# Gated-MLP layer's values: 128-column weight blocks stationary, or token tiles stationary with 512 weight columns moving

## The chip, the cores and the metric

The kernel runs on one core of one Trainium2 chip. The metric is the device time of one execution in microseconds (us). One execution is also recorded by the hardware profiler; its span, from the first to the last instruction of the program, is what the profile's times are measured in.

## The reference, cut to what matters

The reference is one inference step of a two-layer decoder trunk for a prompt group (256 tokens) and a sample group (8 sequences of 8 tokens), 320 tokens in all, `D_MODEL` 1024, in float32. The first layer is a chunked gated MLP:

```python
def chunk_spatial_gating(x, w_in, ln_g, ln_b, w_s, b_s, w_out):
    h = jax.nn.gelu(x @ w_in)                 # w_in: 1024 x 4096
    u, v = jnp.split(h, 2, axis=-1)           # 2048 columns each
    ... # v: layer norm over its 2048 columns
    mixed = jnp.einsum('gts,bnsgd->bntgd', ws, vc) + b_s[:, :L].T[:, :, None]
    y = (u * mixed.reshape(bsz, s, D_A)) @ w_out
    return y, v
```

`x` has been through an RMS norm. The change concerns `v`, the second half of `x @ w_in`: 320 tokens by 2048 columns, 1024 deep. `v` is wanted with tokens on partitions, since the layer norm runs along its columns and the mixing over tokens contracts it. Behind this layer stand a gated convolution MLP, an mLSTM layer and a second convolution MLP; they are not changed.

## The kernel before, in words

**Precision by parts.** A float32 product is made of three float32r matmuls. Each operand is split into a high part (a cast to float32r) and a low part (what is left): `wh`, `wl` of a weight block, `xh`, `xl` of the activations. The products high by high, high by low and low by high are added in PSUM.

**Weights.** All weights are queued by `weights()` in the order of use, as pieces of up to 8 tiles of 128 x 128. `take()` hands out the next piece; `prefetch(n, m)` issues the loads up to piece n (SyncE's queue, SP, into one of 4 `raw` buffers) and the splits up to piece m (ScalarE, ACT, casts `wh`; VectorE, DVE, subtracts to make `wl`; 3 buffers each). Loads run 4 pieces ahead, splits one.

**A block.** `block()` computes 128 output columns for all tokens: for each of the 8 k tiles it calls `self.mm` (L47) three times with a 128 x 128 weight tile stationary and 320 token columns moving, into one PSUM bank `pm` (pool `psm`, 3 banks). TensorE (PE) instructions are pinned in program order; a scheduler places the rest.

**The start.** `run()` loads the activations `xT` (128 partitions x 8 x 320) in four transfers of two k tiles, each followed by a piece of the first weight block (2, 2 and 4 k tiles, then 4 of the second block). After each, `norm_block` makes `xh` and `xl`: the square root of the mean is not yet known, so the parts are of x times the norm's gain, and the row factor `rc` is applied after the matmul. Ten matmuls on ones (`pw`) stand ahead. The squares for the norm follow in block 1, `norm_cols` (row factor by token, `rc`) in block 3, `norm_row` (the same as a row, `rb`) in block 5, `row_sums` in block 10.

**The values.** Sixteen blocks, weight columns 2048 to 4095. Each result has columns on partitions, and is turned: DVE copies it from PSUM to `vT`, and one block later `v_nat` transposes three token tiles (128, 128, and the last 128 tokens, of which the upper 64 are the sample) on PE into `pvt` (three banks of the pool `psa`, which has 5). After four blocks ACT applies gelu with `rc` as scale into `v`, and DVE takes `bn_stats` for the layer norm. The last transposes stand after the first u block.

**After that.** Sixteen blocks for `u`, with the normalising of `v` and the mixing (`mix`) between them, then the output projection.

Of the kernel before, what the change touches and what calls it, by code (L numbers as in the profile page):

```python
# [22 lines left out]
KD = D // P  # L23
DA = 2048
# [9 lines left out]
V_MIX, V_FFN, V_FIN, V_GN, V_LG, V_LB, V_CB, V_FB, V_FW, V_CW = 0, 16, 32, 40, 56, 72, 88, 104, 148, 280  # L34
# [3 lines left out]
class Net:  # L38
# [23 lines left out]
    def weights(self):  # L62

        I = self.I
        q = []

        def add(w, b, *groups, k0=0):
            for kn in groups:
                q.append((w, b, k0, kn))
                k0 += kn  # L70

        add(I["a_win"], 16, 2, 2, 4)
        add(I["a_win"], 17, 4, 4)
        for b in [*range(18, 32), *range(16)]:
            add(I["a_win"], b, 8)
        for b in range(KD):
            add(I["a_wo"], b, 8, 8)

        def ffn(l):
            for b in range(2 * KF):  # L80
                add(I["f_up"][l], b, 8)
            for b in range(KD):
                add(I["f_dn"][l], b, 8, 7, 7)

        ffn(0)
        add(I["b_wg"], 0, 8)
        for h in range(NH):
            for r in range(6):
                if (h, r) == (NH - 1, 4):
                    add(I["b_wo"], 0, 4, k0=8)  # L90
                    add(I["b_wo"], 1, 6, k0=8)
                add(I["b_win"], 6 * h + r, 8)
                for b in self.EARLY_OUT.get((h, r), ()):
                    add(I["b_wo"], b, 8)
        add(I["b_wo"], 2, 6, k0=8)
        add(I["b_wo"], 0, 4, k0=12)
        for b in (1, 2):
# [10 lines left out]
    def prefetch(self, n, m):  # L108

        nc = self.nc  # L110
        while len(self.loaded) < min(n, len(self.wq)):
            w, b, k0, kn = self.wq[len(self.loaded)]
            raw = self.wraw.tile([P, 8, P], F32, tag="raw", name="raw")
            nc.sync.dma_start(raw[:, :kn, :], w[b, :, k0:k0 + kn, :])
            self.loaded.append(raw)
        while len(self.halved) < min(m, len(self.wq)):
            i = len(self.halved)
            raw, kn = self.loaded[i], self.wq[i][3]
            self.loaded[i] = None
# [9 lines left out]
            self.last_split = nc.scalar.copy(wh[:, :kn, :], raw[:, :kn, :])  # L129
            self.last_low = nc.vector.tensor_tensor(wl[:, :kn, :], raw[:, :kn, :], wh[:, :kn, :].bitcast(F32), op=SUB)  # L130
            self.halved.append((wh, wl))
# [89 lines left out]
    def norm_row(self):  # L221
# [13 lines left out]
        nc.scalar.copy(rb, pb[:, :T])  # L235
        self.rb = rb

    def x_rhs(self, k):
        return self.xh[:, k, :], self.xl[:, k, :]

# [14 lines left out]
    def layer_a(self):  # L255
        nc, tc, I, O = self.nc, self.tc, self.I, self.O
        with tc.tile_pool(name="ya", bufs=1) as yp, tc.tile_pool(name="la", bufs=1) as lp:
            yh = yp.tile([P, KA, T], F32R, name="yh_a")
            yl = yp.tile([P, KA, T], F32R, name="yl_a")
            v = lp.tile([P, 3, DA], F32, name="v_a")  # L260
            st = lp.tile([P, 3, 4, 6], F32, name="st_a")
            mv = lp.tile([P, 3, 2], F32, name="mv_a")
# [6 lines left out]
            pvt = {}  # L269

            def load_ws():
                nc.sync.dma_start(ws, I["a_ws"])
# [11 lines left out]
                    self.mm(pr, self.ones, ws[:, 4 * i:4 * i + 4, :], True, True)  # L284
                    nc.scalar.copy(rsum[:, 4 * i:4 * i + 4, :].rearrange("p g t -> p (g t)"), pr)

            def v_nat(b, vT):
                q, c = b // 4, b % 4
                if c == 0:
                    pvt[q] = [self.psa.tile([P, 512], F32, tag="pa", name="pvt") for _ in range(3)]  # L290
                for t in range(3):
                    self.tr(pvt[q][t][:, c * P:(c + 1) * P], self.tokens(vT, t), self.ident)
                if c == 3:
                    for t in range(3):
                        vv = v[:, t, q * 512:(q + 1) * 512]
                        nc.scalar.activation(vv, pvt[q][t], AF.Gelu_apprx_tanh, scale=self.rc[:, t:t + 1])
                        nc.vector.bn_stats(st[:, t, q, :], vv)

            prev = None
            for b in range(16):  # L300
                ps = self.block(KD, self.x_rhs)
                if b == 1:
# [3 lines left out]
                if b == 3:  # L306
                    self.norm_cols()
                    load_ws()
                if b == 5:
                    self.norm_row()  # L310
                if b == 10:
                    row_sums()
                if prev is not None:
                    v_nat(b - 1, prev)
                prev = lp.tile([P, T], F32, tag="vT", name="vT", bufs=2)
                nc.vector.tensor_copy(prev, ps[:, :T])

            ve = lp.tile([P, 3], F32, name="ve_a")
            rs = lp.tile([P, 3], F32, name="rstd_a")

            def v_stats():
                for t in range(3):
                    nc.vector.bn_aggr(mv[:, t, :], st[:, t])
                nc.vector.tensor_scalar(ve, mv[:, :, 1], EPS, None, op0=ADD)
                nc.gpsimd.tensor_tensor(rs, ve, self.mhalf.to_broadcast([P, 3]), op=ALU.pow)
                nc.vector.scalar_tensor_tensor(ve, mv[:, :, 0], -1.0, rs, op0=MULT, op1=MULT)

            def normalise(q):
                for t in range(3):
                    vv = v[:, t, q * 512:(q + 1) * 512]  # L330
                    nc.scalar.activation(vv, vv, AF.Identity, scale=rs[:, t:t + 1], bias=ve[:, t:t + 1])

            def v_rows(q):
                cs = slice(q * 512, (q + 1) * 512)
# [30 lines left out]
            for b in range(16):  # L365
                ps = self.block(KD, self.x_rhs)
                if b == 0:
                    v_nat(15, prev)
# [596 lines left out]
    def run(self):  # L965
        nc, tc, I, O = self.nc, self.tc, self.I, self.O
        with tc.tile_pool(name="const", bufs=1) as cp, tc.tile_pool(name="xp", bufs=1) as xp, \
# [6 lines left out]
            self.xh = xp.tile([P, KD, T], F32R, name="xh")  # L974
# [11 lines left out]
            for i in range(10):  # L986
                self.mm(pw[:, :P], self.ones, self.ones, True, True)
            nc.sync.dma_start(self.vecs[:, :16], I["vecs"][:, :16])
            for i in range(4):
                nc.sync.dma_start(self.xT[:, 2 * i:2 * i + 2, :], I["xT"][:, 2 * i:2 * i + 2, :])  # L990
                self.prefetch(i + 1, 0)
                for m in (2 * i, 2 * i + 1):
                    self.norm_block(m, V_MIX)
                self.prefetch(i + 1, min(i + 1, 3))
            nc.sync.dma_start(self.ident, I["ident"])
            nc.sync.dma_start(self.vecs[:, 16:], I["vecs"][:, 16:])
            self.layer_a()
            self.ffn(0, V_MIX + 8)
            self.layer_b()
# [15 lines left out]
def _lay_out(i):  # L1015
    a = {}
# [5 lines left out]
    a["a_win"] = _blocks(i["a_w_in"][0])  # L1022
# [16 lines left out]
    w = i["b_w_in"][0]  # L1039
# [68 lines left out]
```

## Time and profile before

| | |
|---|---|
| median of 3 runs | 977.2 us (976.13 to 979.38) |
| profiled execution | 977.89 us, its span 975.8 us |
| mean granted TensorE clock in it | 0.994 |
| PE busy | 957.5 us (98%) |
| DVE busy | 686.7 us (70%) |
| ACT busy | 484.6 us (50%) |
| first matmul of the first value block | 5.57 us |
| first matmul of the first u block | 73.27 us |

How to read the profile: PE is the matmul engine, PEld its weight loads, which overlap the matmuls. A row of the timeline gives the start, the length, the engine, the line of the kernel, the operation, `out<-in` by tile names, the shapes and a count. PE's records of neighbouring matmuls overlap, so the pace of a stream is read from start to start. In a row of grouped instructions the numbers behind the bar are busy time, mean ns of one, and the idle time of the engine ahead of them with what ended it. A float32 matmul that is not a transpose shows as two records. A row of the windows gives the stretch, its length, busy time and count by engine, the granted clock, the mean busy share of the DMA engines and GB/s.

### The profile page before, as it was taken

Reading aid. Unit: us, or ns where it says so; the run is one execution under the profiler, and the core shown is the slowest. Engines: PE = TensorE matmul, PEld = TensorE weight load, DVE = VectorE, ACT = ScalarE, POOL = GpSimd, SP = SyncE. Lnnn points to the kernel's source line nnn. Section 1 sums busy time; section 2 is a strip of 40 time slices with the busy share of each in tenths; the row PEclk is TensorE's granted clock in tenths of the full one; section 3 lists DMA queues with packets and bytes.
Section 4 is the critical chain, followed back from the end, with each engine's and each line's share of the span. In section 5 each row is a group of like instructions: output and inputs, shape, how many; then the busy total and the mean of one; then the engine's idle time right before and its main releaser. Section 6 shows DMA issues by size and latency. Waiting matters only on the chain. (4 is left out here: it accounts for less than half of the span.)

```text
span 975.8 us, 17507 instructions
## 1 busy us (share of the span) xinstructions
PE 957.5 (98%) x6703; PEld 941.0 (96%) x6703; DVE 686.7 (70%) x1344; ACT 484.6 (50%) x846; POOL 71.9 (7%) x238
## 2 busy tenths in 40 slices
PE   9999999999999999999989999999999999999996
PEld 8999999999999999999889999999899999999996
DVE  6647985577777764548988887787787777775442
ACT  6437444445554543347456665464565455544332
POOL 0200000010000000012200110011001000000000
PEclk9999999999999999999999999999999999999999
DMA  8534434434444445553854556545273444444441
GB/s 283 193 119 159 140 133 155 152 133 149 151 152 151 148 147 152 150 190 101 279 188 156 189 174 221 170 160 164 73 239 137 152 152 151 152 146 149 147 129 54
DMA packets 55944, 154.73 MB, mean 159 GB/s; under 512 B 6758, under 2 KB 17638, under 8 KB 55862
## 3 DMA queue, kind: packets, MB, share of 16 engines
q1 hardware_dynamic: 55862, 153.62, 47.4%
q8 instruction: 53, 0.87, 0.4%
q14 instruction: 29, 0.24, 0.1%
HBM read 141.66 MB, written 11.94 MB: 157 GB/s over the span
## 5 line engine op out<-in xcount | busy, mean ns | idle before, releaser
L129 ACT CAST wh<-raw 128x1024 fp32r<-128x1024 f32 (+3 forms) x254 | 257.4, 1014 | 353.0 <-PE pm L47 221.9
L47 PE MATMUL pm<-xh,wh 128*128 128x320 f32 x1344 | 422.7, 315 | 1.2 <-ACT wh L129 1.2
L47 PE MATMUL pm<-xh,wl 128*128 128x320 f32 x1344 | 417.5, 311 | 0.1
L47 PE MATMUL pm<-xl,wh 128*128 128x320 f32 x1344 | 417.0, 310 | 0.0
L130 DVE TENSOR_TENSOR wl<-raw,wh 128x1024 fp32r<-128x1024 f32 (+3 forms) x254 | 300.2, 1182 | 124.5 <-ACT wh L129 122.4
L47 PEld LDWEIGHTS pm<-xh,wh 128*128 128x128 f32 x1344 | 253.9, 189 | 2.4 <-ACT wh L129 1.6
L47 PEld LDWEIGHTS pm<-xh,wl 128*128 128x128 f32 x1344 | 253.6, 189 | 0.7 <-DVE wl L130 0.7
L47 PEld LDWEIGHTS pm<-xl,wh 128*128 128x128 f32 x1344 | 253.9, 189 | 0.2
L47 PE MATMUL pm<-yh_f,wh 128*128 128x320 f32 x352 | 109.1, 310 | 0.0
L47 PE MATMUL pm<-yl_f,wh 128*128 128x320 f32 x352 | 108.6, 309 | 0.0
L47 PE MATMUL pm<-yh_f,wl 128*128 128x320 f32 x352 | 108.6, 309 | 0.0
L47 PEld LDWEIGHTS pm<-yl_f,wh 128*128 128x128 f32 x352 | 66.2, 188 | 0.0
L47 PEld LDWEIGHTS pm<-yh_f,wh 128*128 128x128 f32 x352 | 66.1, 188 | 0.0
L47 PEld LDWEIGHTS pm<-yh_f,wl 128*128 128x128 f32 x352 | 66.1, 188 | 0.0
L420 DVE SCALAR_TENSOR_TENSOR fcv<-fpad,vecs,fcv 128x336 f32<-128x336 f32 x88 | 49.6, 566 | 2.2 <-ACT fcv L418 0.7
L243 DVE TENSOR_TENSOR xT<-pm,xT 128x320 f32<-128x320 f32 x40 | 19.6, 491 | 41.6 <-PE pm L47 41.4
L47 PE MATMUL pm<-yhb,wh 128*128 128x320 f32 x128 | 40.3, 315 | 0.2 <-ACT yhb L839 0.2
L47 PE MATMUL pm<-ylb,wh 128*128 128x320 f32 x128 | 39.6, 310 | 0.4 <-DVE ylb L840 0.4
L47 PE MATMUL pm<-yhb,wl 128*128 128x320 f32 x128 | 39.5, 309 | 0.5 <-DVE wl L130 0.5
L47 PE MATMUL pm<-yh_a,wh 128*128 128x320 f32 x128 | 39.6, 309 | 0.0
L47 PE MATMUL pm<-yl_a,wh 128*128 128x320 f32 x128 | 39.5, 309 | 0.0
L47 PE MATMUL pm<-yh_a,wl 128*128 128x320 f32 x128 | 39.5, 309 | 0.0
(241 smaller groups left out, 1116.1 us busy)
## 6 DMA issues: line engine op xcount, KB each, us to landing
raw<-in_f_up SPq DMA_DIRECT2D x88, 512.0 KB, 3.2
raw<-in_b_win SPq DMA_DIRECT2D x48, 512.0 KB, 3.6
raw<-in_a_win SPq DMA_DIRECT2D x30, 512.0 KB, 3.2
raw<-in_f_dn SPq DMA_DIRECT2D x32, 448.0 KB, 3.3
C<-in_C SPq DMA_DIRECT2D x32, 258.0 KB, 5.3
raw<-in_a_wo SPq DMA_DIRECT2D x16, 512.0 KB, 3.7
raw<-in_f_dn SPq DMA_DIRECT2D x16, 512.0 KB, 3.4
out_Cs<-C SPq DMA_DIRECT2D x32, 256.0 KB, 3.9
```

The source lines that it names most:

```text
L47: self.pin(self.nc.tensor.matmul(out, lhsT, rhs, start=start, stop=stop))
L129: self.last_split = nc.scalar.copy(wh[:, :kn, :], raw[:, :kn, :])
L130: self.last_low = nc.vector.tensor_tensor(wl[:, :kn, :], raw[:, :kn, :], wh[:, :kn, :].bitcast(F32), op=SUB)
L243: self.nc.vector.tensor_tensor(x, ps[:, :T], x, op=ADD)
L420: nc.vector.scalar_tensor_tensor(cv, pd[:, i:i + NC], self.vec(w + i * KF), cv, op0=MULT, op1=ADD)
```

## The change

The operands of the value product change places. A tile of 128 tokens of `xh` or `xl` is stationary, and 512 columns of the weights move, so that the result has tokens on partitions and needs no transposes. There are four groups of 512 columns. In a group, for each k tile, two prompt tiles take three matmuls each. The 64 sample tokens take two: `xh` holds behind its 320 token columns a copy (by GpSimd, POOL) of the sample's `xl`, so that 128 stationary columns are the sample's high and low parts side by side (`xs`); they take `wh`. The high 64 alone take `wl`, into the same lower half of the bank. ACT then copies the lower 64 rows of the bank to SBUF, and DVE adds the upper 64. A group holds two banks of `psa` and one of `psm`; gelu reads them as `pvt` before.

The value weights have a layout of their own, `a_wv` (group, partition, k tile by four column tiles), and are taken by k: in the first group 8 pieces of one k tile, in the others 4 pieces of two. At the start `bring` loads `xT` in eight transfers of one k tile, each followed by its weight piece, and `enter` makes that k tile's `xh`, `xl` and copy, while the first group is under way. The loads run no further ahead than that (`AHEAD` 0) until the last x. The squares follow the first group, `norm_cols` and the first group's gelu stand in the middle of the second, `norm_row` after the second, `row_sums` after the third; the statistics for the sample are taken on partitions 64 to 127 alone.

```diff
-        add(I["a_win"], 16, 2, 2, 4)
-        add(I["a_win"], 17, 4, 4)
-        for b in [*range(18, 32), *range(16)]:
+        for g in range(4):
+            add(I["a_wv"], g, *(1,) * 8 if g == 0 else (2,) * 4)
+        for b in range(16):
             add(I["a_win"], b, 8)
...
+    def bring(self, n):
+        nc, I = self.nc, self.I
+        for m in range(self.brought, min(n, KD)):
+            nc.sync.dma_start(self.xT[:, m, :], I["xT"][:, m, :])
+            self.prefetch(m + 1, 0)
+            if m == KD - 1:
+                nc.sync.dma_start(self.ident, I["ident"])
+                nc.sync.dma_start(self.vecs[:, 16:], I["vecs"][:, 16:])
+                self.AHEAD = Net.AHEAD
+        self.brought = max(self.brought, min(n, KD))
+
+    def enter(self, m):
+        self.norm_block(m, V_MIX)
+        self.nc.gpsimd.tensor_copy(self.xx[:, m, T:], self.xl[:, m, TP:])
...
-            def v_nat(b, vT):
-                q, c = b // 4, b % 4
-                if c == 0:
-                    pvt[q] = [self.psa.tile([P, 512], F32, tag="pa", name="pvt") for _ in range(3)]
-                for t in range(3):
-                    self.tr(pvt[q][t][:, c * P:(c + 1) * P], self.tokens(vT, t), self.ident)
-                if c == 3:
...
+            def columns(q, k, pv, wh, wl):
+                xs = self.xx[:, k, TP:TP + P]
+                for t in range(2):
+                    xh, xl = self.tokens(self.xh[:, k, :], t), self.tokens(self.xl[:, k, :], t)
+                    self.mm(pv[t], xh, wh, k == 0, False)
+                    self.mm(pv[t], xl, wh, False, False)
+                    self.mm(pv[t], xh, wl, False, k == KD - 1)
+                if k == 0:
+                    self.mm(pv[2], xs, wh, True, False)
+                self.mm(pv[2][:64], xs[:, :64], wl, False, False)
+                if k > 0:
+                    self.mm(pv[2], xs, wh, False, k == KD - 1)
+
+            def v_gelu(q, pv):
+                cs = slice(q * 512, (q + 1) * 512)
+                r = slice(64, P)
+                vs = lp.tile([P, 512], F32, tag="vs", name="vs", bufs=2)[r]
+                nc.scalar.copy(vs, pv[2][:64])
+                nc.vector.tensor_tensor(vs, vs, pv[2][r], op=ADD)
+                for t in range(2):
+                    nc.scalar.activation(v[:, t, cs], pv[t], AF.Gelu_apprx_tanh, scale=self.rc[:, t:t + 1])
+                    nc.vector.bn_stats(st[:, t, q, :], v[:, t, cs])
+                nc.scalar.activation(v[r, 2, cs], vs, AF.Gelu_apprx_tanh, scale=self.rc[r, 2:3])
+                nc.vector.bn_stats(st[r, 2, q, :], v[r, 2, cs])
+
+            waiting = None
+            for q in range(4):
+                pv = [self.psa.tile([P, 512], F32, tag="pa", name="pv") for _ in range(2)] + \
+                    [self.psm.tile([P, 512], F32, tag="pm", name="pvs")]
+                k = 0
+                while k < KD:
+                    if q == 0:
+                        self.bring(k + 4)
+                        if k + 1 < KD:
+                            self.enter(k + 1)
+                    (wh, wl), kn = self.take()
+                    wh, wl = [x.rearrange("p (k e) c -> p k (e c)", e=4) for x in (wh, wl)]
+                    for i in range(kn):
+                        columns(q, k + i, pv, wh[:, i, :], wl[:, i, :])
+                    k += kn
+                    if q == 1 and k == 4:
+                        self.norm_cols()
+                        v_gelu(0, waiting)
...
-            for i in range(4):
-                nc.sync.dma_start(self.xT[:, 2 * i:2 * i + 2, :], I["xT"][:, 2 * i:2 * i + 2, :])
-                self.prefetch(i + 1, 0)
-                for m in (2 * i, 2 * i + 1):
-                    self.norm_block(m, V_MIX)
-                self.prefetch(i + 1, min(i + 1, 3))
...
+            self.AHEAD, self.brought = 0, 0
+            self.bring(3)
+            self.enter(0)
+            self.prefetch(1, 1)
```

More of the change, by code (lines that the diff above doesn't have):

```diff
@@ L113, in prefetch @@
             raw = self.wraw.tile([P, 8, P], F32, tag="raw", name="raw")
-            nc.sync.dma_start(raw[:, :kn, :], w[b, :, k0:k0 + kn, :])
+            if w is self.I["a_wv"]:
+                kn *= 4
+                nc.sync.dma_start(raw[:, :kn, :], w[b, :, 4 * k0:4 * k0 + kn, :])
+            else:
+                nc.sync.dma_start(raw[:, :kn, :], w[b, :, k0:k0 + kn, :])
             self.loaded.append(raw)
@@ L118, in prefetch @@
             raw, kn = self.loaded[i], self.wq[i][3]
+            if self.wq[i][0] is self.I["a_wv"]:
+                kn *= 4
             self.loaded[i] = None
@@ L268, in layer_a @@
             bdt = lp.tile([P, 64], F32, name="bdt")
-            pvt = {}
             def load_ws():
@@ L285, in row_sums @@
                     nc.scalar.copy(rsum[:, 4 * i:4 * i + 4, :].rearrange("p g t -> p (g t)"), pr)
-            def v_nat(b, vT):
-                q, c = b // 4, b % 4
-                if c == 0:
-                    pvt[q] = [self.psa.tile([P, 512], F32, tag="pa", name="pvt") for _ in range(3)]
-                for t in range(3):
-                    self.tr(pvt[q][t][:, c * P:(c + 1) * P], self.tokens(vT, t), self.ident)
-                if c == 3:
[L294 to L302, printed above, removed]
+            nc.gpsimd.memset(v[:64, 2, :], 0.0)
+            nc.gpsimd.memset(mv[:64, 2, :], 0.0)
+            def columns(q, k, pv, wh, wl):
[10 more added lines that the diff above has]
+                    self.mm(pv[2], xs, wh, False, k == KD - 1)
@@ new lines, in layer_a @@
+            waiting = None
[16 more added lines that the diff above has]
+                        v_gelu(0, waiting)
+                if q == 0:
@@ L305, in layer_a @@
                             self.square_block(m)
-                if b == 3:
-                    self.norm_cols()
+                if q == 1:
+                    self.norm_row()
                     load_ws()
-                if b == 5:
-                    self.norm_row()
-                if b == 10:
+                if q == 2:
                     row_sums()
[L313 to L316, printed above, removed]
+                if q > 0:
+                    v_gelu(q, pv)
+                waiting = pv
             ve = lp.tile([P, 3], F32, name="ve_a")
@@ L322, in v_stats @@
                 for t in range(3):
-                    nc.vector.bn_aggr(mv[:, t, :], st[:, t])
+                    r = slice(64 if t == 2 else 0, P)
+                    nc.vector.bn_aggr(mv[r, t, :], st[r, t])
                 nc.vector.tensor_scalar(ve, mv[:, :, 1], EPS, None, op0=ADD)
@@ L329, in normalise @@
                 for t in range(3):
-                    vv = v[:, t, q * 512:(q + 1) * 512]
-                    nc.scalar.activation(vv, vv, AF.Identity, scale=rs[:, t:t + 1], bias=ve[:, t:t + 1])
+                    r = slice(64 if t == 2 else 0, P)
+                    vv = v[r, t, q * 512:(q + 1) * 512]
+                    nc.scalar.activation(vv, vv, AF.Identity, scale=rs[r, t:t + 1], bias=ve[r, t:t + 1])
             def v_rows(q):
@@ L973, in run @@
             self.xT = xp.tile([P, KD, T], F32, name="xT")
-            self.xh = xp.tile([P, KD, T], F32R, name="xh")
+            self.xx = xp.tile([P, KD, TP + P], F32R, name="xh")
+            self.xh = self.xx[:, :, :T]
             self.xl = xp.tile([P, KD, T], F32R, name="xl")
@@ L988, in run @@
             nc.sync.dma_start(self.vecs[:, :16], I["vecs"][:, :16])
-            for i in range(4):
-                nc.sync.dma_start(self.xT[:, 2 * i:2 * i + 2, :], I["xT"][:, 2 * i:2 * i + 2, :])
-                self.prefetch(i + 1, 0)
-                for m in (2 * i, 2 * i + 1):
-                    self.norm_block(m, V_MIX)
-                self.prefetch(i + 1, min(i + 1, 3))
-            nc.sync.dma_start(self.ident, I["ident"])
-            nc.sync.dma_start(self.vecs[:, 16:], I["vecs"][:, 16:])
+            self.AHEAD, self.brought = 0, 0
+            self.bring(3)
+            self.enter(0)
+            self.prefetch(1, 1)
             self.layer_a()
@@ L1021, in _lay_out @@
                                "f_conv_w", "b_conv_w")], axis=1))
-    a["a_win"] = _blocks(i["a_w_in"][0])
+    a["a_win"] = _blocks(i["a_w_in"][0][:, :DA])
+    a["a_wv"] = np.ascontiguousarray(
+        i["a_w_in"][0][:, DA:].reshape(KD, P, 4, 4, P).transpose(2, 1, 0, 3, 4)).reshape(4, P, 4 * KD, P)
     a["a_wo"] = _blocks(i["a_w_out"][0])
```

1 line of the change is left out of this document (removed).

## The prediction

> **What bounds the kernel now.** I read the page first, then the busy windows of the stage that is rewritten, then its timeline.
>
> ```profile
> span 975.8 us, 17507 instructions
> PE 957.5 (98%) x6703; PEld 941.0 (96%) x6703; DVE 686.7 (70%) x1344; ACT 484.6 (50%) x846; POOL 71.9 (7%) x238
> 5.57:12.72 7.15, 5.88 (x24) 0.76 0.98 343
> 57.87:61.72 3.85, 3.85 (x30) 1.00 0.14 47
> 80.72:84.24 3.52, 3.52 (x27) 1.00 0.32 120
> ```
>
> TensorE (PE) is busy for 98% of the span. The three windows (length, PE busy, records touched, granted clock, DMA share, GB/s) are the first value block, a later one, and a block of the first half of a_w_in (u block). The later blocks have no idle PE at full clock; the first takes twice as long, with idle time and a clock of 0.76. So two things can change the end: how many PE slots the values need, and how the start is fed. A matmul's record overlaps the next, so I count from start to start.
>
> ```profile
> 57.63 0.49 PE L50 MATMUL pvt<-ident,vT 128*128 128x128 f32 x3
> 57.87 0.40 PE L47 MATMUL pm<-xh,wh 128*128 128x320 f32 x1
> ...
> 61.72 0.39 PE L47 MATMUL pm<-xh,wh 128*128 128x320 f32 x1
> ...
> 73.27 0.39 PE L47 MATMUL pm<-xh,wh 128*128 128x320 f32 x1
> ...
> 80.72 0.31 PE L47 MATMUL pm<-xh,wh 128*128 128x320 f32 x1
> ...
> 84.24 0.31 PE L47 MATMUL pm<-xh,wh 128*128 128x320 f32 x1
> ```
>
> A u block of 24 matmuls of 320 columns takes 84.24 - 80.72 = 3.52 us, 146.7 ns each. A value block has three transposes more and takes 61.72 - 57.87 = 3.85, so the transposes cost 0.33. The last value block ends at 73.27.
>
> **Steady part: removed.** Sixteen blocks at 3.85 us go: 61.6 us of PE, of which 56.3 are 384 matmuls and 5.3 the 48 transposes. Sixteen copies of vT on VectorE (DVE) go too; PE never waited for them in the steady blocks, so they count nothing.
>
> **Steady part: added.** Four groups of 8 k steps of 8 matmuls, 256 in all, each with 512 moving columns. In columns it is a draw: 256 x 512 = 131,072 against 384 x 320 + 48 x 128 = 129,024. What decides is the cost that does not grow with the columns, paid 256 times and not 432. No float32r matmul of 512 columns is in this trace; I extrapolate from 258 and 320.
>
> ```profile
> 502.24 0.28 PE L47 MATMUL num<-vh,Ph 128*128 128x258 f32 x1
> ...
> 503.56 0.28 PE L47 MATMUL pCp<-vh,kgl 128*128 128x258 f32 x1
> ```
>
> Eleven starts of 258 columns lie between 502.24 and 503.56: 120 ns each. The step to 320 costs 26.7 ns for 62 columns, 0.43 ns a column, so 512 columns cost 146.7 + 192 x 0.43 = 229 ns. Lower bound: the flattest slope that the rounding of those two starts allows (121 ns at 258 columns, 0.415 a column) gives 226. Upper bound: in proportion to columns, 146.7 x 1.6 = 235. I take 229, nearest to the two measured float32r rows: 256 x 0.229 = 58.6 us, a gain of 3.0 (1.4 to 3.7).
> The Trainium skill, "TensorE: Matmul & The Clock Gate", section "Back-to-back issue gap", has a gap of N / 2.4 + 2.5 ns, 216 ns for 512; by it the sum would be 3.4 us lower. It gives 136 ns for 320 columns where the trace has 146.7, so the measurement decides.
>
> Row sums, norm_cols and norm_row keep their matmuls, only between other instructions. The weight bytes and the cast and subtract of each weight tile stay; ScalarE (ACT) gets four 64-row copies and loses nothing large, DVE four 64-row adds. What covers them:
>
> ```profile
> 20.00:73.30 53.30, 53.30 (x369) 52.01 (x367) 31.27 (x47) 21.36 (x28) 4.98 (x3) 1.00 0.50 167
> L296 ACT ACTIVATE v_a<-pvt,rc 128x512 f32<-128x512 f32 x9 | 5.5, 683 | 0.0
> ```
>
> In this stage DVE is busy 31.27 of 53.30 us and ACT 21.36, under a PE that is full. The exposed place is a group's turn. A group takes two banks of psa, which has five; with the banks of the norms and row sums between, the second token tile of groups 2 and 3 reuses the bank of the first tile of the group before, and waits for its gelu. That bank is complete five matmuls (1.15 us) before the group ends; the gelu is 0.68 us (L296), and the built order puts it ahead of the sample's copy on ACT. It is done before it is wanted, so I count nothing; if ACT is late by a weight cast as well, two turns cost up to 1.3 us each.
>
> **The start.** Now to the feed.
>
> ```profile
> 4.21 1.01 ACT L174 ACTIVATE xh<-xT,vecs 128x320 fp32r<-128x320 f32 x2 [1.92 <-DMA xT<-in_xT]
> 5.57 0.41 PE L47 MATMUL pm<-xh,wh 128*128 128x320 f32 x1
> 6.76 0.31 PE L47 MATMUL pm<-xh,wl 128*128 128x320 f32 x1
> 6.87 1.01 ACT L174 ACTIVATE xh<-xT,vecs 128x320 fp32r<-128x320 f32 x2 [1.35 <-DMA xT<-in_xT]
> 8.23 0.41 PE L47 MATMUL pm<-xh,wh 128*128 128x320 f32 x1 [1.17 <-ACT wh L129]
> ...
> 2.00:4.00 2.00, 2.00 (x11) 1.00 0.83 221
> 4.00:6.00 2.00, 1.99 (x11) 1.00 0.95 274
> 6.00:8.00 2.00, 0.98 (x5) 1.00 0.96 351
> 8.00:10.00 2.00, 1.75 (x6) 0.65 1.06 381
> 10.00:12.00 2.00, 2.00 (x10) 0.50 0.92 321
> L129 ACT CAST wh<-raw 128x512 fp32r<-128x512 f32 x3 | 1.8, 608 | 0.5 <-DMA raw<-in_a_win 0.5
> L130 DVE TENSOR_TENSOR wl<-raw,wh 128x512 fp32r<-128x512 f32 x3 | 2.0, 682 | 0.0
> ```
>
> The first block takes 7.15 us where 3.52 would do: 3.63 us lost, because two k steps of x feed only six matmuls (0.9 us) and the next x lands at 6.87, and because after that pause the clock is granted at half (0.65, 0.50) until about 12. Now each k step has 8 matmuls of 229 ns, 1.83 us of PE, and needs 164 KB of x and 262 KB of weights: 0.43 MB. By the GB/s column 0.44 MB have come by 4 us, 0.99 by 6, 1.69 by 8, 2.45 by 10 and 3.10 by 12. So 0.43 MB take 1.1 to 1.6 us: the feed is faster than PE, where before it was slower. Step by step: x and weights 0 land as now, so the first matmul starts at 5.6; its third waits for wl until about 6.2, and step 0 ends at 7.6. Pair 1 is in at about 7.3: its 0.87 MB have come by 5.6, and a landing lags behind its bytes (the x used at 6.87 was the end of 0.79 MB, which had come by 5.3, a lag of 1.5). Cast 0.61 and subtract 0.68 make 8.6, and six matmuls more end step 1 near 10.0. From there PE is the limit: six steps of 1.83, end 21.0. Without loss it would be 5.57 + 14.66 = 20.2: 0.8 us lost instead of 3.6, a gain of 2.8. Upper end 3.4, when pair 1 is in at 6.7. Lower end 1.2, when the clock is still granted at half for one stretch like that before, 3.1 us, at a cost of half, 1.6.
> The eight x transfers and eight weight transfers stand on SP's queue where nine stood; its issue is under 0.5 us each, 1 us per step, below 1.83. GpSimd copies 64 columns of xl per step, wanted only after the six prompt matmuls, so that is covered.
>
> **Sum.** -3.0 - 2.8 = -5.8 us. The profiled execution took 977.89 (span 975.8), which becomes 972.1; the median of the three runs is 977.2, 0.7 lower, so 971.4. For this case alone 970 to 974.6.
>
> **Rivals.** First, the one that ends slower: the 64-wide stationary. Where the shape of the stationary changes, PE does not overlap:
>
> ```profile
> 494.72 0.31 PE L47 MATMUL pm<-xh,wl 128*128 128x320 f32 x1
> 494.96 1.08 PE L47 MATMUL num<-C,Qz 128*32 128x258 f32 x16
> ```
>
> The 32-wide matmul starts 0.24 us after the 320-column one instead of 0.147, 0.07 before the record's end. A record grows from 0.28 (258) to 0.31 (320), so to 0.40 at 512; the next would start after 0.33, not 0.229: 0.10 us a change. The 32 matmuls that load only xs[:, :64] stand each between 128-wide ones: 64 changes, 6.2 us, net +0.4: 977.6. It decides if over 58 of 64 changes pay. Against it: in the built program these loads are 64 wide but still select all four column groups of the array, as the 128-wide ones do, while the loads of num select one. I give it 0.12.
> The Trainium skill, "TensorEngine Tiling (Array Packing)", "Key Properties", says that changing the tiling mode drains TensorE, and the row agrees, with 0.09 us. "PSUM — Partial Sum Buffer", "The four PSUM rules", of the same skill says that float32r matmuls force the column group to all; no run here shows that yet.
>
> Second, the start stays as lossy as it is: x in single steps and more transfers land no earlier, the clock drops, 3.6 us are lost again. For it: the half clock in the rows above. Against it: the bytes. Time 977.2 - 3.0 = 974.2; chance 0.12. Third, the turns, two of 1.3 us: 971.4 + 2.6 = 974.0, or 976.8 if the start is lossy as well. For it: PE then waits in program order, with everything behind. Against it: the order of the gelus and the idle share of ACT. Chance 0.08. That the change doesn't do what it says (the transposes stay, say) is excluded by the built order: 256 matmuls of 512 columns and no transposes in this stage.
>
> **Numbers.** Forecast 0.68, the switch 0.12, the start 0.12, the turns 0.08. A measurement here tells about 0.3%, 2.9 us, from no change. Below 974.3 lie 0.65 of the forecast's 0.68 and just under half of the start and the turns together (0.09 of 0.20): faster 0.74. Within 0.3% lie the upper edge of the forecast, the rest of those two, and most of the switch, 0.08: same 0.20 (0.03 + 0.09 + 0.08). A switch with a lossy start, 977.6 + 2.8 = 980.4, is slower: 0.04, and 0.02 for a start and turns beyond their prices: 0.06. The range leaves out the switch and reaches from 969.8, 0.3 under the forecast's low end for the spread of runs, to the turns with a lossy start, 976.8.
>
> **What would show it.** Starts of 512-column rows 226 to 235 ns apart, first u block at 67 to 69 us instead of 73.27, the first group over at 21, no clock of 0.5 at 8 to 12. Wrong if rows next to the 64-wide ones start 0.33 apart (switch), if group 0 ends after 23 (start), or if PE waits for ACT at the start of group 2 or 3 (turns).

## The result, and the profile after

The changed kernel takes 970.58 us (median of 4 runs, 970.23 to 972.09) where the kernel before takes 977.18 (976.13 to 979.38): a ratio of 0.9933, 95% interval 0.9919 to 0.9947. The forecast was 971.4. The profiled execution took 970.37, with a span of 968.6.

The first lines of the page, and then one row from the busy windows of PE (length, PE busy, records) for the first group, 5.63 to 21.20:

```profile
span 968.6 us, 17160 instructions
PE 951.8 (98%) x6527; PEld 922.9 (95%) x6527; DVE 684.6 (71%) x1333; ACT 489.8 (51%) x851; POOL 75.1 (8%) x248
5.63:21.20 15.57, 15.57 (x66) 11.56 (x66) 9.34 (x16) 9.35 (x17) 2.62 (x7) 1.00 0.95 306
```

PE is as full as before; 5.7 us of its busy time are gone. In the first group, where the old first block stood idle and half-clocked, the window counts no idle PE and a clock of 1.00. Its start is not free of loss all the same: the first two steps take 4.55 us, two later ones 3.67.

The timeline of PE, start of the first group, then a later step, then the start of the second group and the end of the stage:

```profile
5.63 0.60 PE L47 MATMUL pv<-wh,xh 128*128 128x512 f32 x1
6.06 0.40 PE L47 MATMUL pv<-wh,xl 128*128 128x512 f32 x1
6.35 0.50 PE L47 MATMUL pv<-wl,xh 128*128 128x512 f32 x1
...
7.97 0.50 PE L47 MATMUL pv<-wh,xh 128*128 128x512 f32 x1
8.31 0.40 PE L47 MATMUL pv<-wh,xl 128*128 128x512 f32 x1
8.70 0.50 PE L47 MATMUL pv<-wl,xh 128*128 128x512 f32 x1
...
10.18 0.39 PE L47 MATMUL pv<-wh,xh 128*128 128x512 f32 x1
...
14.55 0.39 PE L47 MATMUL pv<-wh,xh 128*128 128x512 f32 x1
14.78 0.39 PE L47 MATMUL pv<-wh,xl 128*128 128x512 f32 x1
15.01 0.39 PE L47 MATMUL pv<-wl,xh 128*128 128x512 f32 x1
15.23 0.40 PE L47 MATMUL pvs<-wl,xh 128*64 128x512 f32 x1
15.47 0.39 PE L47 MATMUL pvs<-wh,xh 128*128 128x512 f32 x1
15.70 0.40 PE L47 MATMUL pv<-wh,xh 128*128 128x512 f32 x1
...
21.20 0.40 PE L47 MATMUL pv<-wh,xh 128*128 128x512 f32 x1
21.43 0.40 PE L47 MATMUL pv<-wh,xl 128*128 128x512 f32 x1
22.01 0.50 PE L47 MATMUL pv<-wl,xh 128*128 128x512 f32 x1 [0.18 <-DVE wl L136]
...
68.41 0.39 PE L47 MATMUL pvs<-wh,xh 128*128 128x512 f32 x1
68.64 0.31 PE L47 MATMUL pm<-xh,wh 128*128 128x320 f32 x1
```

Step 0 ends at 7.97 and step 1 at 10.18; from there a step takes 1.83 to 1.84 us, 229 ns from start to start. The row behind the 64-wide stationary starts 0.24 after it, the others 0.22 to 0.23. Behind the first steps, one wait for weights is visible, at 22.01: the first weights of the second group are split late, and the two starts around it are 0.58 apart, not 0.23. The first group is over at 21.20, and the first u block begins at 68.64 (73.27 before).

**Where the 7.2 us of span went.** The stage gives 4.63, and 0.33 more because no transposes stand behind the first u block: 5.0. At the first matmul of the output projection the changed kernel leads by as much, 135.65 against 140.68, and it holds that lead for 295 us:

```profile
140.68 0.40 PE L47 MATMUL pm<-yh_a,wh 128*128 128x320 f32 x1
```

```profile
135.65 0.39 PE L47 MATMUL pm<-yh_a,wh 128*128 128x320 f32 x1
```

The next 1.6 come at the turn from the first convolution MLP to the mLSTM layer, which the change does not touch: the lead is 5.0 in front of it and 6.6 behind. The timeline of PE there, of the kernel before:

```profile
433.37 0.61 PE L47 MATMUL pc<-ones,acc 128*128 128x2 f32 x4
435.22 0.58 PE L47 MATMUL pc<-ones,acc 128*128 128x2 f32 x2 [1.24 <-DVE acc L210]
435.67 0.61 PE L47 MATMUL pm<-xh,wh 128*128 128x320 f32 x1
436.08 0.47 PE L47 MATMUL pm<-xl,wh 128*128 128x320 f32 x1
...
438.72 0.31 PE L47 MATMUL pm<-xh,wl 128*128 128x320 f32 x1
438.87 0.31 PE L47 MATMUL pm<-xh,wh 128*128 128x320 f32 x1
```

and of the changed kernel:

```profile
428.33 0.61 PE L47 MATMUL pc<-ones,acc 128*128 128x2 f32 x4
430.19 0.38 PE L47 MATMUL pc<-ones,acc 128*128 128x2 f32 x2 [1.25 <-DVE acc L216]
430.43 0.39 PE L47 MATMUL pm<-xh,wh 128*128 128x320 f32 x1
430.66 0.31 PE L47 MATMUL pm<-xl,wh 128*128 128x320 f32 x1
```

Both pause for the same 1.24 or 1.25 us. Behind the pause, the kernel before runs at 267 ns a matmul instead of 147 until 438.7, and the changed kernel does not. The busy window over that stretch shows a granted clock of 0.50:

```profile
435.26:438.68 3.42, 3.42 (x13) 3.42 (x14) 0.89 (x5) 1.04 (x1) 0.85 (x1) 0.50 0.84 271
```

The last 0.6 come at the first `num<-C` matmuls, whose wait for the transfer of C is that much shorter in this trace. It is not a part of the change: the stretch that holds this wait, from the matmuls that spread the row factor (`pb`) to the second start of `pcs`, takes 57.10 us in the kernel before and 56.53 in the changed kernel here, but 57.26 in a second trace of the changed kernel and 56.94 and 57.68 in two traces of the kernel before with a filled pause elsewhere. So the stage accounts for 5.0 of the 7.2 us of span, and 2.2 were made elsewhere.

The time of an execution is longer than its span, and by less in the changed kernel: by 1.7 to 1.8 us in each of its ten unaltered runs, against 2.0 to 2.1 in the runs of the kernel before. These 0.3 us are a part of the measured gain that no trace shows; what makes them stays open.

### The profile page after: what moved, and what is told of

Read it like the earlier page. It is cut to its first block, busy times and chain, and to the rows that moved or that the text cites. A ratio compares the mean times of both kernels' runs of the same rounds, so it can differ in the third digit from the quotient of the medians.

```text
span 968.6 us, 17160 instructions
## 1 busy us (share of the span) xinstructions
PE 951.8 (98%) x6527; PEld 922.9 (95%) x6527; DVE 684.6 (71%) x1333; ACT 489.8 (51%) x851; POOL 75.1 (8%) x248
## 5 line engine op out<-in xcount | busy, mean ns | idle before, releaser
L47 PE MATMUL pm<-xh,wh 128*128 128x320 f32 x1216 | 379.6, 312 | 0.0
L47 PE MATMUL pm<-xh,wl 128*128 128x320 f32 x1216 | 375.8, 309 | 0.0
L47 PE MATMUL pm<-xl,wh 128*128 128x320 f32 x1216 | 375.7, 309 | 0.0
L47 PEld LDWEIGHTS pm<-xh,wh 128*128 128x128 f32 x1216 | 228.4, 188 | 0.8
L47 PEld LDWEIGHTS pm<-xl,wh 128*128 128x128 f32 x1216 | 228.4, 188 | 0.3
L47 PEld LDWEIGHTS pm<-xh,wl 128*128 128x128 f32 x1216 | 228.2, 188 | 0.0
```

The source lines that it names most:

```text
L47: self.pin(self.nc.tensor.matmul(out, lhsT, rhs, start=start, stop=stop))
```

## The experiments

The ratios are against the kernel before, run on the same chip beside them (977.75 us for the first four experiments, 976.26 for the next four, 977.65 for the last two). My theory: a fixed cost for each matmul makes the steady part cheaper, and transfers in single k steps that each feed 1.83 us of PE make the start cheaper. The rivals: fine transfers alone do it; the 64-wide stationary costs much; the rest of the 6.6 us belongs to the change as well.

**Coarse start.** `xT` in four transfers of two k tiles, the first group's weights in four pieces of two; the parts of two k tiles are made ahead of each piece.

```diff
-            add(I["a_wv"], g, *(1,) * 8 if g == 0 else (2,) * 4)
+            add(I["a_wv"], g, *(2,) * 4)
...
-            nc.sync.dma_start(self.xT[:, m, :], I["xT"][:, m, :])
-            self.prefetch(m + 1, 0)
+            nc.sync.dma_start(self.xT[:, m:m + 2, :], I["xT"][:, m:m + 2, :])
+            self.prefetch(m // 2 + 1, 0)
```

> The changed kernel, but x comes in four transfers of two k tiles and the first group's weights in four pieces of two k tiles (512 KB), as the old start had its x. The products are the new ones. Theory (the start's gain needs both, small first steps and more PE work for each byte of x): the first pair is 0.33 MB of x and 0.52 MB of weights, in at about 7.2 us instead of 4.9; the first matmul comes at 8.2 instead of 5.63, the first group ends at 23.6 to 25.5 instead of 21.20 (the upper end if the clock is granted at half for one stretch of 3.4 us after the pause), and the whole is 2.4 to 4.3 us slower than the changed kernel: 973 to 975. Rival (the new products alone repair the start, since PE then has 1.8 us of work per k step): the first group still ends by 22, 970.6 to 971.4.

974.67 us, ratio 0.9966 (0.9954 to 0.9978). The timeline of PE:

```profile
7.79 0.79 PE L47 MATMUL pv<-wh,xh 128*128 128x512 f32 x1 [2.00 <-ACT wh L135]
...
10.06 0.63 PE L47 MATMUL pv<-wh,xl 128*128 128x512 f32 x1
10.49 0.63 PE L47 MATMUL pv<-wl,xh 128*128 128x512 f32 x1
...
25.55 0.40 PE L47 MATMUL pv<-wh,xh 128*128 128x512 f32 x1
```

The first matmul waits 2.2 us longer, for the larger first weight piece; then a stretch runs 0.43 us a matmul, the pace of half clock, until 13.8. The clock column of the windows has 1.00 there, so it does not show this stretch. The first group is over at 25.55 instead of 21.20, 4.35 later; the first u block starts at 72.52, 3.9 later, since the weight wait of 22.01 is absent. Without the fine steps the new blocks lose the whole 2.7 of the start and 1.7 us more, half of it as a later first matmul, the rest in the slow stretch.

**Fine start, old blocks.** The kernel before, with `xT` in eight transfers and the first block's weights in eight pieces of one k tile.

```diff
-        add(I["a_win"], 16, 2, 2, 4)
+        add(I["a_win"], 16, *(1,) * 8)
...
+    def first_block(self):
+        ps = self.psm.tile([P, 512], F32, tag="pm", name="pm")
+        for k in range(KD):
+            self.bring(k + 4)
+            if k + 1 < KD:
+                self.norm_block(k + 1, V_MIX)
+            self.chunk(ps, lambda j: self.x_rhs(k + j), k == 0, k == KD - 1)
+        return ps
```

> The kernel before, its sixteen blocks and transposes unchanged, but fed as the changed one: x in eight transfers of one k tile, block 16 in eight pieces of one k tile, the parts of x made one step ahead inside the first block. Theory (small steps alone give little, since a step of 0.23 MB comes in 0.6 to 0.9 us and feeds three matmuls, 0.44 us): PE waits at every step, the last x is in at about 9, the first block ends at 11 to 12.3 instead of 12.72, the steady blocks stay at 3.85 us; 975.5 to 977. Rival (the gain of the start is the finer transfers): first block over by 10.1, 974.3 to 974.6.

981.26 us, ratio 1.0045 (1.0029 to 1.0061): slower, a clear miss. The timeline of PE:

```profile
9.96 0.41 PE L47 MATMUL pm<-xh,wh 128*128 128x320 f32 x1 [0.32 <-ACT wh L129]
...
12.11 0.41 PE L47 MATMUL pm<-xh,wh 128*128 128x320 f32 x1 [0.47 <-ACT wh L129]
...
12.94 0.47 PE L47 MATMUL pm<-xh,wl 128*128 128x320 f32 x1
14.43 0.63 PE L47 MATMUL pm<-xh,wh 128*128 128x320 f32 x1 [1.02 <-ACT wh L129]
```

and two of its busy windows:

```profile
14.00:16.00 2.00, 1.57 (x5) 1.35 (x6) 1.32 (x2) 0.99 (x2) 0.00 (x0) 0.50 0.98 371
16.00:18.00 2.00, 2.00 (x10) 2.00 (x9) 0.86 (x1) 1.94 (x4) 0.00 (x0) 0.50 0.97 344
```

An old step has 0.44 us of PE work against 1.83 in the new one. PE drains it and waits for the next cast, over and over; the last matmul of the first block starts at 12.94 (12.58 before). The second block then starts at 14.43 (12.72 before): its first weights are cast only at 13.76, when they have landed, since this kernel too asks for them behind the last x. And the clock is at half for two stretches, 12.4 to 19.3. So the fine transfers alone gain nothing. That this is for the small step alone is not shown: the feed was slower as well, 2.2 MB by 12 us by the GB/s column against 3.1 in the kernel before, with first weight pieces of 66 KB where the new ones have 262. Neither half of the edit brings the start's gain alone.

**Halves.** Each 512-column matmul as two of 256.

```diff
+            def halves(out, lhsT, rhs, start, stop):
+                self.mm(out[:, :256], lhsT, rhs[:, :256], start, False)
+                self.mm(out[:, 256:], lhsT, rhs[:, 256:], False, stop)
```

> The changed kernel, but each matmul of 512 moving columns is made as two of 256 with the same stationary: 512 matmuls and as many weight loads instead of 256, the columns the same. Theory (a matmul costs about 0.43 ns a column and some 9 ns besides, so the gain of the steady part is the number of matmuls): 119 ns a start as for 258 columns, 61.0 us instead of 58.7, 2.3 us slower, 972.5 to 973.5. Rival (only columns count, the steady gain is the transposes' alone): 114.5 ns a start and no change, 970.6.

974.37 us, ratio 0.9962 (0.9947 to 0.9977). The first u block:

```profile
71.12 0.30 PE L47 MATMUL pm<-xh,wh 128*128 128x320 f32 x1
```

That is 2.48 us later than in the changed kernel, for 256 more matmuls of the same columns: 9.7 ns each. Start and waits are not quite alike in the two traces; a steady k step alone takes 1.908 us instead of 1.833, 9.3 ns for each matmul more. The number of matmuls does cost by itself, about the 2.3 us that were expected. The median is 3.8 over the changed kernel's, and 0.9 over the expected 973.5; the profiled execution also met a half clock at the turn (433.8 to 437.2), of which more below.

**All 128 columns for the sample's `wl`.** No 64-wide stationary is left; the upper half of that bank then takes the low by low product as well.

```diff
-                self.mm(pv[2][:64], xs[:, :64], wl, False, False)
+                self.mm(pv[2], xs, wl, False, False)
```

> The changed kernel, but the sample's product with wl takes all 128 columns of xs (high and low part) instead of the high 64, so no stationary is 64 wide; the low part's product with wl, a term of the order of the rounding, is added besides. Theory (a 64-wide load costs what a 128-wide one does, and no change of the array's shape is paid): starts stay at 226 to 236 ns, 970 to 971.5, no change. Rival (each of the 64 changes of width costs 0.1 us, or a narrow load is cheaper): 6 us faster, or 0.5 us slower.

971.65 us, ratio 0.9936 (0.9921 to 0.9951). The spacing is 226 to 227 ns throughout, 3.627 us for 16 matmuls instead of 3.667. One 64-wide use costs 0.040 / 2 = 20 ns, and all 32 of them 0.64 us. The switch rival's price was 200 ns a use. The first u block comes at 67.73; 0.48 of the 0.91 us is the weight wait of 22.01, which is absent here.

**The changed kernel again.** Was that wait a part of the change?

> The changed kernel again, unaltered, beside the next three. Theory (of the 7.2 us between the first two spans 5.0 belong to the value stage and 1.4 to one stretch of 3.4 us at half clock at the turn to the mLSTM layer, which falls by the phase of the clock's windows): the first u block again at 68.2 to 68.8 us; the stretch at the turn may come or not; 970 to 972. Rival (the turn is faster because of the change): never a half clock at the turn in this kernel.

971.18 us, ratio 0.9946 (0.993 to 0.9962). First u block at 68.26, no wait at the second group, no half clock at the turn. Instead PE waits 0.43 us for a cast in front of the second step. The wait at the second group comes and goes with the landing of the transfers: the cast that stood behind a transfer until 19.64 starts at 18.44 here.

**128 columns, and two small loads later.** As the all-128 kernel, with the transfers of `ident` and `vecs[:, 16:]` moved behind the middle of the second group.

```diff
             if m == KD - 1:
-                nc.sync.dma_start(self.ident, I["ident"])
-                nc.sync.dma_start(self.vecs[:, 16:], I["vecs"][:, 16:])
                 self.AHEAD = Net.AHEAD
...
                     if q == 1 and k == 4:
+                        nc.sync.dma_start(self.ident, I["ident"])
+                        nc.sync.dma_start(self.vecs[:, 16:], I["vecs"][:, 16:])
                         self.norm_cols()
```

> The changed kernel with the sample's wl product over all 128 columns (as in the run before) and with the transfers of the identity and the later gain columns (0.23 MB) moved from the end of the start to the middle of the second group. Theory (64-wide matmuls cost 20 ns more each, 0.64 us in all; the wait of 0.5 us for wl at the second group's start is its weights landing late behind those transfers): no wait at the second group, starts all 227 ns, first u block at 67.4 to 67.8 instead of 68.64, 0.9 us faster than the changed kernel on average. Rival (both are chance): 68.2 to 68.7.

971.16 us, ratio 0.9937 (0.9922 to 0.9952). First u block at 67.34, the earliest of all; the first group over at 20.80. The 0.9 to 1.3 us of the stage do not show in the median. In its trace the stretch that holds the wait for C, named above, takes 57.45 us, 0.9 more than in the changed kernel's first trace.

**The turn filled.** The same kernel, with five matmuls on ones in the pause at the turn.

```diff
         for t in range(3):
+            if twice and t == 2:
+                for i in range(5):
+                    self.mm(pc[:, 256:384], self.ones, self.ones, True, True)
```

> The kernel of the run before this one, with five matmuls on ones (1.07 us) put into the 1.24 us for which TensorE waits for VectorE at the turn to the mLSTM layer. Nothing else is changed. Theory (that pause, when it falls into one window of the clock, costs 3.4 us at half clock, about 1.4 us): no half clock at the turn in the profile, never slower than without them, on average 0.3 to 1 us faster, the highest run below 971. Rival (the half clock has another cause): the stretch still comes in about half the runs.

969.93 us (969.16 to 971.06), ratio 0.9931 (0.9915 to 0.9947); the lowest median of the study, though its interval covers the changed kernel's. The timeline of PE at the turn:

```profile
427.10 0.61 PE L47 MATMUL pc<-ones,acc 128*128 128x2 f32 x4
427.57 1.36 PE L47 MATMUL pc<-ones 128*128 128x128 f32 x10
428.96 0.38 PE L47 MATMUL pc<-ones,acc 128*128 128x2 f32 x2
429.20 0.39 PE L47 MATMUL pm<-xh,wh 128*128 128x320 f32 x1
```

The pause is gone, nothing starts later for it, and the clock stays full. From the first `pg` matmul to the row factor it is 8.44 us, as in the unfilled kernels that escape the half clock (8.43 to 8.49), against 9.96 to 9.99 in those that meet it. So the half-clock stretch costs 1.5 us. That the filling kept it away is not shown by this trace: its turn lies against the clock's windows (last section) as in unfilled kernels that escape.

**Before, with its first block filled.** Was the start's loss the clock's or the feed's? Six and two matmuls on ones stand in the two pauses of the first block.

```diff
+            if self.used in (1, 2):
+                for i in range(6 if self.used == 1 else 2):
+                    self.mm(self.pw[:, :P], self.ones, self.ones, True, True)
```

> The kernel before with its old start, and eight matmuls on ones put into the pauses of the first value block (six behind the first piece of two k tiles, two behind the second). They add nothing to the result. Theory (3.6 us are lost in the first block, about 2.1 as pauses and 1.5 as 3.4 us at half clock that the pause brings on): full clock from 5 us on, first block over at 10.8 to 11.6 instead of 12.72, first u block at 71.4 to 72.2 instead of 73.27, 975.2 to 976.5, 1.5 us faster than before. Rival (the half clock does not hang on the pause): over at 12.7 or later, no gain.

976.44 us, ratio 0.9994 (0.9983 to 1.0006). The timeline of PE:

```profile
9.86 0.42 PE L47 MATMUL pm<-xh,wh 128*128 128x320 f32 x1
10.11 0.31 PE L47 MATMUL pm<-xl,wh 128*128 128x320 f32 x1
10.59 0.42 PE L47 MATMUL pm<-xh,wl 128*128 128x320 f32 x1 [0.17 <-DVE wl L130]
...
12.15 0.31 PE L47 MATMUL pm<-xh,wh 128*128 128x320 f32 x1
```

The clock is full from the start to the turn, but the first block is over at 12.15, only 0.57 earlier: a miss, 10.8 to 11.6 were expected. The third piece's weights are split no earlier, so a faster PE reaches them and waits. Nor does the full clock here show that the filling works. The trace of the next experiment, the kernel before with a filled turn, has the old start unfilled, with much the same pause, and full clock all the same:

```profile
8.31 0.41 PE L47 MATMUL pm<-xh,wh 128*128 128x320 f32 x1 [1.07 <-ACT wh L129]
...
12.37 0.31 PE L47 MATMUL pm<-xh,wh 128*128 128x320 f32 x1
```

There the first block is over at 12.37 and the first u block starts at 72.90, both some 0.4 earlier than in the kernel before. So of the 3.63 us that the old start loses, the feed takes some 3 and the half clock 0.4 to 0.6.

**Both kernels with the turn filled.** The same five matmuls, in the kernel before and in the changed kernel.

> The kernel before, with five matmuls on ones in TensorE's pause while the third token tile's sum is made, at the turn from the first convolution MLP to the mLSTM layer (0.6 us of work in a pause of 1.24 us). The profile should show no half clock there and 8.4 to 8.5 us from the first projection of that turn to the row factor, where before has 9.97. Theory: before meets the half clock there in most of its executions, and loses 1.5 us by it; then the median is 1.0 to 1.5 us under that of the kernel before, 975.5 to 976.2. Rival: it comes in few executions of either kernel and the whole difference of 6.6 us was made in the value stage; then the median does not move, 976.5 to 977.5.

> The changed kernel with the same five matmuls at the same turn. Theory: the changed kernel meets the half clock there in few of its executions; the median stays at 970.3 to 971.0 and the difference to the other kernel of this call is 5.0 to 5.6 us, what the traces show for the value stage and the transfer of C. Rival, the clock has nothing to do with it: the difference of the two filled kernels stays 6.6 us.

Before, filled: 976.13 us (975.44 to 979.41), ratio 0.999 (0.998 to 1.0001). Changed, filled: 971.23 (969.91 to 972.71), ratio 0.9931 (0.9916 to 0.9946), 0.2 over what was expected. The medians lie 4.9 apart, nearer to the stage's 5.0 than to 6.6, but the intervals are too wide to settle it. In the trace the filled turn keeps full clock in both. Only the changed one tests the filling, since its turn lies whole in one window of the clock (0.8 to 2.7 us from the window's start), as in the unfilled kernels that meet the half clock; the other is cut by a boundary. In the changed one, the half clock comes 60 us later instead, behind another pause, which every kernel here has:

```profile
490.48 0.38 PE L47 MATMUL pcs<-vh,kz 32*128 32x256 f32 x1 [1.36 <-DVE vl L761]
...
492.28 0.47 PE L47 MATMUL pm<-xh,wh 128*128 128x320 f32 x1
492.54 0.47 PE L47 MATMUL pm<-xl,wh 128*128 128x320 f32 x1
```

The mean granted clock of every run in this study says more. (The end of each execution, where PE is done, stands at half in both kernels; 0.997 or more leaves hardly room for another such stretch.) With 0.997 or more, the kernel before takes a median of 975.93 us (15 runs, 975.44 to 976.79) and the changed kernel 970.32 (4 runs, 970.01 to 970.73): 5.6 us apart. With 0.994 or less, the kernel before takes 978.56 (16 of 53 runs), the changed kernel 973.79 (1 of 10). At 0.996 alone the medians are 977.36 (15 runs) and 971.63 (5 runs), 5.7 apart. So the times of each kernel go with the clock that it happens to be granted, by some 3 us, and at the same clock the two are 5.6 to 5.7 apart. Two traces at such a clock, the kernel before with the filled turn and the second of the changed kernel, again have 5.0 between them at the output projection (140.31 and 135.26). With the 0.3 outside the span that makes 5.3; the rest is not placed.

## Why the prediction was right, and where it was not

**Steady part: right in size, and in mechanism for one half.** 229.2 ns from start to start, as extrapolated from 258 and 320 columns; 256 x 0.2292 = 58.7 us against 61.6, a gain of 2.9 (forecast 3.0). The Trainium skill ("TensorE: Matmul & The Clock Gate", "Back-to-back issue gap") gives 216 ns for an isolated matmul of 512 columns; this stream does not agree. Without the 64-wide rows it is 227, so that the agreement to the nanosecond is partly luck. That each matmul has a cost whatever its columns is shown by the halves, at 9 to 10 ns. But it is not all of the gain. An estimate from the rows: the 384 old matmuls (56.3 us) have the columns of 240 new ones (55.0), a gain of 1.3. The other 1.6 come from 48 transposes (5.3 us) giving way to the 16 matmuls that are left (3.7): a transpose took 110 ns for its 128 columns, some 45 more than 10 ns and 0.43 ns a column would make.

**Start: right in size, with one wrong reason.** The first group ends at 21.20 (forecast 21.0) and the gain is 2.66 (forecast 2.8). The steps hold: pair 1 in at 7.29 (7.3), step 1 over at 10.18 (10.0), PE the limit from there. The coarse start and the fine start with old blocks show that neither the new blocks nor the fine transfers bring it alone; that the larger step is what makes the fine transfers pay is argued from the rows, since the old blocks' weight pieces were smaller too. Wrong was how the half clock was priced, at half of its stretch, 1.6, for the lower end: filled, the old start gained 0.57, and at full clock by chance some 0.4, because a faster PE only waits longer for weights.

**Turns: right.** PE waits for no gelu at groups 2 and 3. Not foreseen was the wait for `wl` at the second group, 0.48 us in one of the two traces of this kernel.

**The switch: refuted.** The 64-wide use costs 20 ns, not 200. That fits "PSUM — Partial Sum Buffer", "The four PSUM rules", of the Trainium skill, that float32r forces the column group to all, so that the 64-wide loads are no change of tiling.

**The sum: right in total, by parts that offset.** Forecast -5.8; the stage gave -5.0 in the trace. Of the 0.8 that is missing there, 0.48 is the weight wait, 0.14 the start, and 0.1 the pace. The rest of what was measured (6.6 by the medians, 7.2 by the spans) was not in my steps: between the two profiled executions the clock at the turn (1.6) and the wait for C (0.6), and in every run the 0.3 outside the span. At equal high clock the difference is 5.6, 0.2 from the forecast; the rest of the 6.6 goes with the clock that the runs were granted. Even that closeness is partly luck: the 0.3 outside the span were not forecast, and a mean of 0.997 leaves hardly room for the half clock of the old start, 0.4 to 0.6 us that the forecast had counted as gained. That I took the profiled execution of before as one time, without asking what in it was chance, is the step that was missing: its trace had a stretch of half clock 430 us behind the start, in a place that the edit does not touch.

## What to carry to other kernels

Where PE is full, count matmuls as well as columns: with a new 128-wide float32r stationary each, a matmul costs some 10 ns beside its columns here, so that 512 wide beats 320 wide even at equal columns, and transposes left out can be worth as much. Before the first transfers are split finely, ask whether each piece feeds PE for as long as the next takes to come; the split into single k tiles came with a start 2.7 us shorter where a step had 1.83 us of work, and made the stage 4.1 us longer (77.41 against 73.27) where it had 0.44. And before a few us are put down to an edit, line the two traces up along PE and see where the lead grows: here 2 of 7 us came from places that the edit never touched.

## What the hardware showed that was not expected

**The clock at a pause is a matter of phase.** In every trace here the granted clock is 1.0 or 0.5 and its stretches, but for the last, which the end cuts off, are multiples of 3.413 us. That agrees with the Trainium skill, "TensorE: Matmul & The Clock Gate", "What's actually happening", which has windows of 3413 ns that run free of the kernel. The moments at which the clock changes give the window's grid in each trace, and the pause at the turn can be placed on it. What counts as low there is taken from the first of the four `pc` matmuls on `acc` to the end of the wait, 1.85 us in before. Positions are in us from the start of a window, worked out from the traces:

| kernel, turn not filled | low stretch | half clock after it |
|---|---|---|
| before | 1.5 to 3.4 | yes |
| halves | 0.5 to 2.3 | yes |
| all 128 columns | 0.9 to 2.8 | yes |
| before, first block filled | 0.5 to 2.4 | yes |
| changed | 2.6 to 1.1 of the next | no |
| changed again | 3.2 to 1.6 of the next | no |
| coarse start | 2.0 to 0.5 of the next | no |
| fine start, old blocks | 1.8 to 0.3 of the next | no |
| 128 columns, late loads | 2.9 to 1.3 of the next | no |

The four that meet the half clock have the whole stretch in one window; the five that escape have it cut in two by a boundary. The same holds for the later pause, in front of `pcs`: with the short matmuls on both sides it is a stretch of 2.4 us, which lies in one window (0.2 to 2.6) in the changed kernel with the filled turn alone, the only one of twelve traces with a half clock there. So a change in the first 70 us that moves a pause 400 us later against this grid can win or lose 1.5 us there. Of the three filled turns, two are cut by a boundary (3.2 to 1.7 of the next) and would by this rule have escaped unfilled; the one in the changed kernel is whole (0.8 to 2.7) and kept full clock. That filling helps rests on this one trace.

No run set the phase on purpose; the rule is read from these traces, and for these two pauses alone. It does not cover the old start: there a pause of 1.17 us that ends at 8.23, inside one window, brought the half clock, and the pause of 1.07 us that ends at 8.31, shown with the filled first block, also inside one window, did not.

**The prices of a matmul**, each with a new float32r stationary of 128 columns, from start to start: 120 ns for 256 or 258 columns moving, 146.7 for 320, 227 for 512, and 20 ns more for each 64-wide stationary among them.
